# Row variance over 8192 columns: from chunk statistics on VectorE to a two-pass form, with the last two tiles' loads cut smaller

## Chip, cores, metric

One core of one Trainium2 chip. The metric is device time in microseconds of one execution, smaller is better. "Span" is the core's time in a profiled execution; in the runs here the measured time is 1.7 to 2.2 us above it. Runs of one call (one build, one chip, one sitting) agree within about 0.15%.

## The reference

```python
def setup_inputs():
    return {"x": np.random.randn(8192, 8192).astype(np.float32)}

def reference(x):
    return np.var(x, axis=1)
```

268 MB have to be read once and 32 KB written.

## The kernel before

A tile is 128 partitions of 2 rows each, 8.39 MB. There are 32 tiles and three tile buffers. For each row VectorE takes statistics of twelve 512-column chunks, ScalarE sums the last 2048 columns and their squares around the first chunk's mean, GpSimd turns these into a thirteenth entry, and VectorE aggregates.

```python
    data = ctx.enter_context(tc.tile_pool(name="data", bufs=3))
    # ... J = 2, F = 512, C = 16, AC = 4, DC = 12, NA = 2048
    def row_stats(xt, j):
        # ...
        for c in range(DC):
            bn(st, c, xt[:, o + c * F : o + (c + 1) * F])
        k = st[:, 1:2]
        src = xt[:, o + DC * F : o + m]
        nc.scalar.activation(out=junk, in_=src, func=ACTF.Identity, bias=k, scale=-1.0,
                             accum_out=s12[:, 0:1])
        nc.scalar.activation(out=junk, in_=src, func=ACTF.Square, bias=k, scale=-1.0,
                             accum_out=s12[:, 1:2])
        # ... six small GpSimd operations, then bn_aggr on VectorE (finish)
    for t in range(NT - 1):
        xt = data.tile([P, J * m], FP32, name="xt")
        nc.sync.dma_start(out=xt, in_=x_t[t])              # one load a tile
        # ... row_stats for both rows, finish one row later
    # last tile: row 0 whole, row 1 in pieces
    nc.sync.dma_start(out=xt[:, 0:m], in_=x_t[t, :, 0:m])
    pieces = [4096, 2048, 1024, 512, 256, 256]
    # ... row 0 as above, row 1 in 17 chunks on VectorE alone
    with nc.allow_non_contiguous_dma(reason="two values per partition"):
        nc.sync.dma_start(out=out_last[t], in_=var_last)   # 128 writes of 8 bytes
```

## Time and profile before

| | before |
|---|---|
| time, median | 648.35 us (648.18 to 649.04, 4 runs) |
| span of the profiled run | 646.7 us |
| last piece of the input landed | 629.2 us |
| VectorE done | 642.5 us |

The prediction shows the profile's lines. The table's third line is not on the page: it is from the trace's record of the semaphores that loads raise, where each load shows sixteen steps, one for each of the 16 DMA engines by my reading (the trace does not name them). The sixteenth step is taken as the landing: the last load's first step is at 622.49, its sixteenth at 629.20. The view of stretches puts the end in two lines (columns: stretch in us and its length, then busy us and number of instructions of PE, PEld, DVE, ACT and POOL, TensorE's clock, DMA share, GB/s):

```profile
609.60:629.20 19.60, 0.42 (x1) 0.12 (x1) 19.54 (x34) 12.46 (x13) 2.15 (x13) 1.00 0.66 273
629.20:642.60 13.40, 0.42 (x1) 0.13 (x1) 13.27 (x25) 0.42 (x3) 0.56 (x3) 1.00 0.01 2
```

After 629.2 nothing comes in any more (2 GB/s), and VectorE is busy for 13.27 of 13.4 us. That is the part of a load-bound kernel that can be shortened.

### The profile page before, as it was taken

The numbers are of one execution on the slowest core, as the hardware profiler recorded it, in microseconds if no ns is written. First come the engines' busy times: TensorE is split into PE (matmuls) and PEld (weight loads), VectorE is DVE, ScalarE is ACT, GpSimd is POOL, SyncE is SP. The second block draws the span as 40 slices with busy tenths as digits, with TensorE's granted clock in tenths as the row PEclk, the third lists the DMA queues.
The fourth block names the chain that finished last, engine by engine and source line by source line (L and its number), as shares of the span: only waits on it lengthen the run. The fifth ranks groups of instructions, "written<-read, shape, count | busy, mean of one in ns | idle before, by whom it ended". The sixth has DMA issues, their size and how long they took to land.

```text
span 646.7 us, 1908 instructions
## 1 busy us (share of the span) xinstructions
PE 0.8 (0%) x2; PEld 0.3 (0%) x2; DVE 485.3 (75%) x838; ACT 265.5 (41%) x255; POOL 58.9 (9%) x384
## 2 busy tenths in 40 slices
PE   0000000000000000000000000000000000000000
PEld 0000000000000000000000000000000000000000
DVE  0576797776897776887767987677977677976797
ACT  0443455343454342454343554333553434552450
POOL 0010110010100010101010100101100101100110
DMA  9999999999999999999999999999999999999950
GB/s 389 454 417 426 454 426 417 454 439 405 450 446 401 450 450 398 450 450 409 438 446 422 430 442 439 409 450 454 397 450 446 401 450 446 398 447 454 395 209 3
DMA packets 5663, 268.59 MB, mean 415 GB/s; under 512 B 753, under 2 KB 1040, under 8 KB 1296
## 3 DMA queue, kind: packets, MB, share of 16 engines
q1 hardware_dynamic: 5648, 268.47, 96.2%
q14 instruction: 15, 0.12, 0.1%
HBM read 268.44 MB, written 0.03 MB: 415 GB/s over the span
## 4 chain that ended last, share of the span: by engine, by line
DMA 72%; DVE 26%; issue 1%; SPq 0%; DVEq 0%
DMA xt<-in_x_dram 72%; DVE st L50 25%; DVE stl L50 1%; DVE mv L127 0%; DVE mv L78 0%; DVE mv L124 0%; SPq L84 0%; DVEq L50 0%; DVE var_last L128 0%
## 5 line engine op out<-in xcount | busy, mean ns | idle before, releaser
L50 DVE BATCH_NORM_STATS2 st<-xt 128x6 f32<-128x512 f32 x756 | 451.6, 678 | 157.2 <-DMA xt<-in_x_dram 157.2
L63 ACT ACTIVATE junk<-xt,st 128x2048 f32<-128x2048 f32 x63 | 124.2, 1971 | 339.4 <-DVE st L50 339.4
L65 ACT ACTIVATE junk<-xt,st 128x2048 f32<-128x2048 f32 x63 | 124.2, 1971 | 2.0
L69 POOL TENSOR_SCALAR tmp<-s 128x1 f32<-128x1 f32 x63 | 12.0, 190 | 387.9 <-ACT junk L63 387.9
L78 DVE BATCH_NORM_AGGREGATE mv<-st 128x2 f32<-128x75 f32 x62 | 25.8, 457 | 0.0
L73 POOL TENSOR_TENSOR st<-s,tmp 128x1 f32<-128x1 f32 x63 | 11.9, 189 | 100.6 <-ACT junk L65 100.6
L79 POOL COPY var_all<-mv 128x1 f32<-128x1 f32 x62 | 11.4, 183 | 79.0 <-DVE mv L78 79.0
L71 POOL TENSOR_TENSOR st<-st,tmp 128x1 f32<-128x1 f32 x63 | 11.9, 189 | 5.2
L72 POOL TENSOR_TENSOR tmp<-s,tmp 128x1 f32<-128x1 f32 x63 | 11.9, 189 | 0.0
L63 ACT ACTIVATION_READ_ACCUMULATOR junk<-xt,st 128x1 f32 x63 | 11.7, 186 | 0.0
L65 ACT ACTIVATION_READ_ACCUMULATOR junk<-xt,st 128x1 f32 x63 | 11.7, 186 | 0.0
L63 ACT ACT_TABLE_LOAD x1 | 1.3, 1283 | 22.7 <-DMA xt<-in_x_dram 22.7
L50 DVE BATCH_NORM_STATS2 stl<-xt 128x6 f32<-128x512 f32 (+1 forms) x17 | 9.6, 645 | 0.0
L68 POOL MEMSET st<- 128x1 f32 x63 | 6.2, 98 | 0.3 <-POOLq L145 0.3
L110 ACT COPY vs<-vp 31x128 f32<-31x128 f32 x2 | 0.5, 254 | 3.3 <-PE vp L109 3.3
L109 PE MATMUL vp<-ident,var_all 128*31 128x128 f32 x2 | 0.8, 420 | 631.7 <-POOL var_all L79 631.7
L127 DVE BATCH_NORM_AGGREGATE mv<-stl 128x2 f32<-128x102 f32 x1 | 0.6, 616 | 0.0
L109 PEld LDWEIGHTS vp<-ident,var_all 128*31 128x31 f32 x2 | 0.3, 126 | 632.0 <-POOL var_all L79 632.0
L124 DVE BATCH_NORM_AGGREGATE mv<-st 128x2 f32<-128x75 f32 x1 | 0.5, 481 | 0.0
L125 POOL COPY var_last<-mv 128x1 f32<-128x1 f32 x1 | 0.2, 183 | 1.3 <-DVE mv L124 1.3
masks.py:199 POOL TENSOR_SCALAR_AFFINE_SELECT ident<-ident 128x128 f32<-128x128 f32 x1 | 0.3, 292 | 0.1
masks.py:197 POOL MEMSET ident<- 128x128 f32 x1 | 0.2, 204 | 0.0
(5 smaller groups left out, 0.6 us busy)
## 6 DMA issues: line engine op xcount, KB each, us to landing
xt<-in_x_dram SPq DMA_DIRECT2D x1, 4096.0 KB, 34.9
xt<-in_x_dram SPq DMA_DIRECT2D x1, 2048.0 KB, 39.5
xt<-in_x_dram SPq DMA_DIRECT2D x1, 1024.0 KB, 41.4
xt<-in_x_dram SPq DMA_DIRECT2D x1, 512.0 KB, 42.2
xt<-in_x_dram SPq DMA_DIRECT2D x31, 44.5
xt<-in_x_dram SPq DMA_DIRECT2D x1, 256.0 KB, 42.4
xt<-in_x_dram SPq DMA_DIRECT2D x2, 128.0 KB, 40.6
out_dram<-vs SPq DMA_DIRECT2D x1, 31.0 KB
```

Of the source, the lines that this page charges most:

```text
L50: nc.vector.bn_stats(out=st[:, at * 6 : at * 6 + 6], in_=src)
L63: nc.scalar.activation(out=junk, in_=src, func=ACTF.Identity, bias=k, scale=-1.0, accum_out=s12[:, 0:1])
L65: nc.scalar.activation(out=junk, in_=src, func=ACTF.Square, bias=k, scale=-1.0, accum_out=s12[:, 1:2])
L68: nc.gpsimd.memset(st[:, b : b + 1], float(NA))
L69: nc.gpsimd.tensor_scalar(out=tmp[:, 0:1], in0=s12[:, 0:1], scalar1=1.0 / NA, scalar2=0.0, op0=ALU.mult, op1=ALU.add)
L71: nc.gpsimd.tensor_tensor(out=st[:, b + 1 : b + 2], in0=k, in1=tmp[:, 0:1], op=ALU.subtract)
L72: nc.gpsimd.tensor_tensor(out=tmp[:, 1:2], in0=s12[:, 0:1], in1=tmp[:, 0:1], op=ALU.mult)
L73: nc.gpsimd.tensor_tensor(out=st[:, b + 2 : b + 3], in0=s12[:, 1:2], in1=tmp[:, 1:2], op=ALU.subtract)
L78: nc.vector.bn_aggr(out=mv, in_=st)
L79: nc.gpsimd.tensor_copy(out=var_all[:, j, t : t + 1], in_=mv[:, 1:2])
L109: nc.tensor.transpose(vp, var_all[:, j, 0 : NT - 1], ident)
L127: nc.vector.bn_aggr(out=mv, in_=stl[:, 0 : i * 6])
```

## The change

The intent: one VectorE instruction sums a row by adding its halves as 4096 pairs, ScalarE divides by the row's length and then sums the squared differences in place. VectorE's work for a tile falls (from 14.34 us for 24 statistics to two sums), so that it is ready when the last pieces come. The last two tiles' loads are cut smaller; the last tile keeps chunk statistics, with 2048 columns of its last row on ScalarE.

```diff
+    def row_sum(s, i, src, w):
+        nc.vector.scalar_tensor_tensor(
+            out=pair[:, 0 : w // 2], in0=src[:, 0 : w // 2], scalar=1.0, in1=src[:, w // 2 : w],
+            op0=ALU.mult, op1=ALU.add, accum_out=s[:, i : i + 1])
+    def row_sq(s, k, src, t, j):
+        # (k == 1)
+        nc.scalar.activation(out=mean, in_=s[:, 0:1], func=ACTF.Identity, scale=1.0 / m)
+        nc.scalar.activation(out=src, in_=src, func=ACTF.Square, bias=mean, scale=-1.0,
+                             accum_out=ssq[:, j, t : t + 1])
     for t in range(NT - 1):
         xt = data.tile([P, J * m], FP32, name="xt")
-        nc.sync.dma_start(out=xt, in_=x_t[t])
+        if last:                                   # tile 30
+            for lo, hi in ((0, m), (m, m + H), (m + H, 2 * m)):
+                nc.sync.dma_start(out=xt[:, lo:hi], in_=x_t[t, :, lo:hi])
+        else:
+            nc.sync.dma_start(out=xt, in_=x_t[t])
         # ... row_sum, row_sq for both rows (the last row of tile 30 in two sums)
-    nc.sync.dma_start(out=xt[:, 0:m], in_=x_t[t, :, 0:m])
-    pieces = [4096, 2048, 1024, 512, 256, 256]
+    for w in [2048] * 6 + [1024, 1024, 512, 512, 512, 256, 256]:
         nc.sync.dma_start(out=xt[:, lo : lo + w], in_=x_t[t, :, lo : lo + w])
         # ... tile 31: row 0 in 16 chunks, row 1 in 13 chunks on VectorE, 2048 columns on ScalarE
```

More of the change, by code (lines that the diff above doesn't have):

```diff
@@ L27 @@
     NT = n // (P * J)
-    C = m // F
-    AC = 4
-    DC = C - AC
-    NA = AC * F
-    T3 = 3
+    H = m // 2
     x_t = x.rearrange("(t p j) f -> t p (j f)", p=P, j=J)
@@ L39 @@
     data = ctx.enter_context(tc.tile_pool(name="data", bufs=3))
-    stats = ctx.enter_context(tc.tile_pool(name="stats", bufs=6))
-    small = ctx.enter_context(tc.tile_pool(name="small", bufs=6))
+    stats = ctx.enter_context(tc.tile_pool(name="stats", bufs=1))
+    small = ctx.enter_context(tc.tile_pool(name="small", bufs=4))
     singles = ctx.enter_context(tc.tile_pool(name="singles", bufs=1))
     psum = ctx.enter_context(tc.tile_pool(name="psum", bufs=1, space=bass.MemoryType.PSUM))
-    var_all = singles.tile([P, J, NT], FP32)
+    ssq = singles.tile([P, J, NT], FP32)
@@ L46 @@
     var_last = singles.tile([P, J], FP32)
-    junk = psum.tile([P, NA], FP32)
-    def bn(st, at, src):
-        nc.vector.bn_stats(out=st[:, at * 6 : at * 6 + 6], in_=src)
-    def row_stats(xt, j):
-        st = stats.tile([P, DC * 6 + T3], FP32)
-        s12 = small.tile([P, 2], FP32)
-        tmp = small.tile([P, 2], FP32)
-        o = j * m
-        for c in range(DC):
-            bn(st, c, xt[:, o + c * F : o + (c + 1) * F])
-        k = st[:, 1:2]
-        src = xt[:, o + DC * F : o + m]
-        nc.scalar.activation(out=junk, in_=src, func=ACTF.Identity, bias=k, scale=-1.0,
-                             accum_out=s12[:, 0:1])
-        nc.scalar.activation(out=junk, in_=src, func=ACTF.Square, bias=k, scale=-1.0,
-                             accum_out=s12[:, 1:2])
-        b = DC * 6
-        nc.gpsimd.memset(st[:, b : b + 1], float(NA))
-        nc.gpsimd.tensor_scalar(out=tmp[:, 0:1], in0=s12[:, 0:1], scalar1=1.0 / NA, scalar2=0.0,
-                                op0=ALU.mult, op1=ALU.add)
-        nc.gpsimd.tensor_tensor(out=st[:, b + 1 : b + 2], in0=k, in1=tmp[:, 0:1], op=ALU.subtract)
-        nc.gpsimd.tensor_tensor(out=tmp[:, 1:2], in0=s12[:, 0:1], in1=tmp[:, 0:1], op=ALU.mult)
-        nc.gpsimd.tensor_tensor(out=st[:, b + 2 : b + 3], in0=s12[:, 1:2], in1=tmp[:, 1:2], op=ALU.subtract)
-        return st
@@ L76, in finish @@
-    def finish(st, t, j):
-        mv = small.tile([P, 2], FP32)
-        nc.vector.bn_aggr(out=mv, in_=st)
-        nc.gpsimd.tensor_copy(out=var_all[:, j, t : t + 1], in_=mv[:, 1:2])
-    pending = []
+    pair = psum.tile([P, H], FP32)
+    ident = singles.tile([P, P], FP32)
+    make_identity(nc, ident)
+    def row_sum(s, i, src, w):
+        nc.vector.scalar_tensor_tensor(
+            out=pair[:, 0 : w // 2], in0=src[:, 0 : w // 2], scalar=1.0, in1=src[:, w // 2 : w],
+            op0=ALU.mult, op1=ALU.add, accum_out=s[:, i : i + 1])
@@ new lines, in row_sq @@
+    def row_sq(s, k, src, t, j):
+        mean = small.tile([P, 1], FP32, name="mean")
+        if k == 1:
+            nc.scalar.activation(out=mean, in_=s[:, 0:1], func=ACTF.Identity, scale=1.0 / m)
+        else:
+            parts = small.tile([P, 4], FP32, name="parts")
+            nc.scalar.activation(out=parts[:, 0:k], in_=s[:, 0:k], func=ACTF.Identity, scale=1.0 / m,
+                                 accum_out=mean)
+        nc.scalar.activation(out=src, in_=src, func=ACTF.Square, bias=mean, scale=-1.0,
+                             accum_out=ssq[:, j, t : t + 1])
@@ L82 @@
     for t in range(NT - 1):
         xt = data.tile([P, J * m], FP32, name="xt")
-        nc.sync.dma_start(out=xt, in_=x_t[t])
-        for j in range(J):
-            st = row_stats(xt, j)
-            pending.append((st, t, j))
-            if len(pending) > 1:
-                finish(*pending.pop(0))
+        rows = [xt[:, j * m : (j + 1) * m] for j in range(J)]
+        last = t == NT - 2
+        if last:
+            for lo, hi in ((0, m), (m, m + H), (m + H, 2 * m)):
+                nc.sync.dma_start(out=xt[:, lo:hi], in_=x_t[t, :, lo:hi])
+        else:
+            nc.sync.dma_start(out=xt, in_=x_t[t])
@@ L92 @@
+        for j in range(J):
+            s = small.tile([P, 2], FP32, name="s")
+            if last and j == J - 1:
+                row_sum(s, 0, rows[j][:, 0:H], H)
+                row_sum(s, 1, rows[j][:, H:m], H)
+                row_sq(s, 2, rows[j], t, j)
+            else:
+                row_sum(s, 0, rows[j], m)
+                row_sq(s, 1, rows[j], t, j)
     t = NT - 1
     xt = data.tile([P, J * m], FP32, name="xt")
-    nc.sync.dma_start(out=xt[:, 0:m], in_=x_t[t, :, 0:m])
-    pieces = [4096, 2048, 1024, 512, 256, 256]
@@ L96 @@
-    lo = m
-    for w in pieces:
+    lo = 0
+    for w in [2048] * 6 + [1024, 1024, 512, 512, 512, 256, 256]:
         nc.sync.dma_start(out=xt[:, lo : lo + w], in_=x_t[t, :, lo : lo + w])
         lo += w
-    st = row_stats(xt, 0)
-    finish(*pending.pop(0))
-    ident = singles.tile([P, P], FP32)
-    make_identity(nc, ident)
     vs = singles.tile([NT - 1, P, J], FP32)
     for j in range(J):
-        vp = psum.tile([NT - 1, P], FP32, name="vp")
-        nc.tensor.transpose(vp, var_all[:, j, 0 : NT - 1], ident)
-        nc.scalar.copy(vs[:, :, j], vp)
+        vp = pair[0 : NT - 1, j * F : j * F + P]
+        nc.tensor.transpose(vp, ssq[:, j, 0 : NT - 1], ident)
+        nc.scalar.mul(vs[:, :, j], vp, 1.0 / m)
@@ L111 @@
     nc.sync.dma_start(out=out_tj[0 : NT - 1], in_=vs)
-    stl = stats.tile([P, (C + 1) * 6], FP32, name="stl")
-    lo, i = m, 0
-    while lo < 2 * m:
-        w = F
-        if 2 * m - lo <= 512:
-            w = 256
-        bn(stl, i, xt[:, lo : lo + w])
-        lo += w
-        i += 1
-        if i == 2:
-            mv = small.tile([P, 2], FP32)
-            nc.vector.bn_aggr(out=mv, in_=st)
-            nc.gpsimd.tensor_copy(out=var_last[:, 0:1], in_=mv[:, 1:2])
-    mv = small.tile([P, 2], FP32)
@@ L127, with bn @@
-    nc.vector.bn_aggr(out=mv, in_=stl[:, 0 : i * 6])
-    nc.vector.tensor_copy(out=var_last[:, 1:2], in_=mv[:, 1:2])
+    def bn(st, i, lo, w):
+        nc.vector.bn_stats(out=st[:, i * 6 : i * 6 + 6], in_=xt[:, lo : lo + w])
+    st0 = stats.tile([P, m // F * 6], FP32, name="st0")
+    for c in range(m // F):
+        bn(st0, c, c * F, F)
+    mv0 = small.tile([P, 2], FP32, name="mv0")
+    NA = 2048
+    st1 = stats.tile([P, 13 * 6 + 3], FP32, name="st1")
+    b = 13 * 6
+    s12 = small.tile([P, 2], FP32, name="s12")
@@ new lines @@
+    tmp = small.tile([P, 2], FP32, name="tmp")
+    nc.gpsimd.memset(st1[:, b : b + 1], float(NA))
+    bn(st1, 0, m, F)
+    k = st1[:, 1:2]
+    src = xt[:, m + NA : m + 2 * NA]
+    junk = pair[:, NA : 2 * NA]
+    nc.scalar.activation(out=junk, in_=src, func=ACTF.Identity, bias=k, scale=-1.0, accum_out=s12[:, 0:1])
+    nc.scalar.activation(out=junk, in_=src, func=ACTF.Square, bias=k, scale=-1.0, accum_out=s12[:, 1:2])
+    nc.gpsimd.tensor_scalar(out=tmp[:, 0:1], in0=s12[:, 0:1], scalar1=1.0 / NA, scalar2=0.0,
+                            op0=ALU.mult, op1=ALU.add)
@@ new lines @@
+    nc.gpsimd.tensor_tensor(out=st1[:, b + 1 : b + 2], in0=k, in1=tmp[:, 0:1], op=ALU.subtract)
+    nc.gpsimd.tensor_tensor(out=tmp[:, 1:2], in0=s12[:, 0:1], in1=tmp[:, 0:1], op=ALU.mult)
+    nc.gpsimd.tensor_tensor(out=st1[:, b + 2 : b + 3], in0=s12[:, 1:2], in1=tmp[:, 1:2], op=ALU.subtract)
+    for i in range(1, 4):
+        bn(st1, i, m + i * F, F)
+    nc.vector.bn_aggr(out=mv0, in_=st0)
+    nc.gpsimd.tensor_copy(out=var_last[:, 0:1], in_=mv0[:, 1:2])
+    lo = m + 2 * NA
+    for i, w in enumerate([512] * 7 + [256, 256]):
+        bn(st1, 4 + i, lo, w)
+        lo += w
@@ L129 @@
+    mv1 = small.tile([P, 2], FP32, name="mv1")
+    nc.vector.bn_aggr(out=mv1, in_=st1)
+    nc.vector.tensor_copy(out=var_last[:, 1:2], in_=mv1[:, 1:2])
     with nc.allow_non_contiguous_dma(reason="two values per partition"):
```

## The prediction

> **What bounds the kernel now.** I read the busy shares first, then the slices, the DMA queues, the chain that ended last, and last the timeline of the end.
>
> ```profile
> PE 0.8 (0%) x2; PEld 0.3 (0%) x2; DVE 485.3 (75%) x838; ACT 265.5 (41%) x255; POOL 58.9 (9%) x384
> ...
> DMA  9999999999999999999999999999999999999950
> ...
> q1 hardware_dynamic: 5648, 268.47, 96.2%
> q14 instruction: 15, 0.12, 0.1%
> ...
> DMA 72%; DVE 26%; issue 1%; SPq 0%; DVEq 0%
> ...
> L50 DVE BATCH_NORM_STATS2 st<-xt 128x6 f32<-128x512 f32 x756 | 451.6, 678 | 157.2 <-DMA xt<-in_x_dram 157.2
> L63 ACT ACTIVATE junk<-xt,st 128x2048 f32<-128x2048 f32 x63 | 124.2, 1971 | 339.4 <-DVE st L50 339.4
> ```
>
> No engine is the bound over the run: VectorE is busy 75%, and waits 157.2 us for loads. The DMA slices stand at 9 until the last two. 268.4 MB of input have to come in, and the queue is full for 96.2% of the span. The 26% that the chain gives VectorE are mostly not worth removing: the chain alternates between a load that waited for a buffer and the VectorE work that freed that buffer, but loads are queued two deep, so that work lies beside transfers. Only the two ends of the span are exposed: the first tile's load (22.7 us until VectorE starts) and whatever follows the last landing.
>
> ```profile
> 565.02 44.55 DMA xt<-in_x_dram
> ...
> 609.66 7.29 DVE st L50 x13
> ...
> 633.39 8.33 DVE stl L50 x15
> 641.72 0.02 issue
> 641.74 0.62 DVE mv L127
> 642.36 0.03 issue
> 642.39 0.15 DVE var_last L128
> ```
>
> From 609.66, when tile 30 (the last but one) is complete, VectorE works without a pause until 642.54. It has 24 chunks of tile 30, 12 of tile 31's row 0 and 17 of row 1 to do, and while VectorE needs 14.34 us for a whole tile plus 0.83 for its aggregates, the arrival of the tile 31 pieces doesn't hold it back at all. The trace's record of the loads' semaphores, which one step per DMA engine raises, says when data was there: the fifteenth engine delivers its last piece of tile 31 at 625.1, the sixteenth and last at 629.2. So 13.3 us of VectorE work stand behind the last landing, and then 4.2 us of output (642.54 to 646.7).
>
> **A second loss, in the same record.** The first engine delivers a tile every 19.35 us. The last engine trails it by 0.55 us at tile 0 and by 6.9 at tile 29, and this grows in seven jumps, the first of 0.6 and the others of about 0.95 us. The packets of the instruction queue (8 KB each, about 0.31 us) fall at such jumps (60.6, 143.7, 241.4, 319.8, 398.2, 495.9, 574.2 us). VectorE has 838 instructions, one jump for each 120. My reading is that VectorE's instruction fetches go through one DMA engine that also carries data, and every tile waits for that engine. This is an inference, not shown.
>
> [...] This trace has no two-input VectorE operation[...]; its 512-column statistic, one input, starts every 14.34/24 = 0.598 us[...].
>
> **The change, main loop.** Removed for tiles 0 to 30: 12 chunk statistics and an aggregate a row on VectorE, two 2048-column activations on ScalarE and six small operations on GpSimd. Added per row: one VectorE sum of 4096 pairs with an accumulator read [...], one tiny ScalarE activation for the mean [...], and one Square over 8192 in place [...]. [...] None of this moves the stream: the main loop gains nothing directly.
>
> **The change, stream.** VectorE drops to 63 sums, 63 accumulator reads, 29 statistics and 3 others, 158 instructions: one fetch after the start instead of seven. ScalarE has about 200. I expect a lag of 1.5 to 2.5 us of the last engine in place of 6.7. Against that stand more pieces: in the trace each load costs the first engine some 0.07 us over its bytes (2048 columns come every 2.49 us, where bytes alone make 2.42), and there are 16 loads for tiles 30 and 31 where there were 8, so +0.6. The first engine ends at 622.5 now, then at 623.1, and the last landing falls at 623.1 + 2 = about 625.0 (now 629.2).
>
> **The change, end.** Tile 29 lands at about 584.8, tile 30 at 604.8.
> - ScalarE: [...] The transposes' copies (each 0.25, and one wait for TensorE) bring 621.3. Then the two 2048 activations for the share of the last row that it took, 2 x 2.15: 625.6. GpSimd's last step 0.5: 626.1.
> - VectorE: [...] Tile 31's row 0 comes in four pieces, 2.49 us apart, with 4 x 0.598 = 2.39 of work each: it keeps pace. In row 1 the second piece is ScalarE's, which gives it about 2.4 us of slack, and the later pieces shrink from 1024 to 256 columns. After the last landing one 256 statistic is left (the 256 form shows 0.416): 625.4.
> - So the last aggregate starts at the later of 625.4 and 626.1, say 626.3. Aggregate 0.62, copy 0.18: 627.1. The output's 4.2: span 631.3, against 646.7. The measured time was 1.8 above the span (648.52 against 646.7): 633.1. Gain 15.2 us: 4.2 from the earlier last landing, 11 from the shorter work behind it.
>
> I predict **633.2 us**, 2.3% below 648.34. The threshold of 2% lies near 635.6.
>
> **Rivals.**
> - [...]
> - **ScalarE becomes the bound of the end.** Its chain from tile 29 is only 0.7 us longer than the loads' in my sum; each 0.3 us more a row makes 1.2 us. [...]
> - **The fetches do not shrink, or the lag has another cause.** Then the last landing is 629.8; VectorE has little behind it: 630.2 + 0.8 + 4.2 + 1.8 = 637.0, 1.7% faster.
> - **The stream gets thin,** since buffers come free later and the piecewise loads wait for earlier semaphores (in the new order the loads after the eighth of tile 31 wait for pieces of that tile itself). Each is still issued over 5 us before its turn, so I expect nothing; if it bites, 1 to 3 us.
>
> **Range and chances.** [...] Together: faster by over 2% 0.68, within 2% 0.30, slower 0.02. The range that should hold eight of ten is 630.5 to 638.
>
> **What would show it.** [...] In the waits, VectorE and ScalarE both wait for loads or for each other in every tile, and the load queue waits for ScalarE with DMA slices still at 9. In the semaphore record, the last engine less than 3 us behind the first. In the timeline, the last Square of tile 30 ending near 620, the ScalarE share near 625.6, and VectorE idle just before its last pieces or its last aggregate. A DMA slice under 9 before the end, or VectorE busy without a pause from tile 30 on, would make the prediction wrong.

The sum came to 633.1 us, written as 633.2. Terms of it: what VectorE takes for the sum of a row, and what ScalarE takes for a row. They led from tile 29's landing (584.8) to the 621.3 of ScalarE's line. The time to spare in the main loop rested on them too, and so did a rival with a slower sum, given 18%, and the split of the chances by it. The trace of the changed kernel shows these terms: 4433 ns for the sum and 141 for its accumulator read, 195 for the mean, 7123 for the Square; from tile 29's first sum to the end of the fourth row it took 34.1 us (585.47 to 619.57).

## The result, and the profile after

634.38 us median (634.12 to 634.73, 4 runs) against 648.35. The ratio is 0.9783 (95% interval 0.9766 to 0.98): faster by 2.2%. Ratios here are the mean time of one kernel's fast runs over the mean of the other's of the same rounds, so not quite the ratio of the medians quoted. A second call with the unaltered changed kernel gave 633.49 us and 0.9765.

The page of the changed kernel: busy shares, slices, queues, chain and the two main groups (their lines end in busy us, mean ns of one, and the engine's idle time before them with what ended it).

```profile
PE 0.8 (0%) x2; PEld 0.3 (0%) x2; DVE 297.2 (47%) x158; ACT 462.4 (73%) x194; POOL 1.6 (0%) x12
...
DMA  9999999999999999999999999999999999999994
...
q1 hardware_dynamic: 6800, 268.47, 98.5%
q14 instruction: 5, 0.04, 0.0%
...
ACT 42%; DMA 40%; DVE 15%; another core or an unknown queue 2%; issue 0%; SPq 0%; DVEq 0%
...
L62 ACT ACTIVATE xt<-xt,mean 128x8192 f32<-128x8192 f32 x62 | 441.6, 7123 | 2.0
L49 DVE SCALAR_TENSOR_TENSOR pair<-xt 128x4096 f32<-128x4096 f32 (+1 forms) x63 | 275.0, 4366 | 328.6 <-ACT xt L62 236.3
```

The last group mixes two widths. The view of the tile `pair` shows its durations apart (ns, shortest/median/longest):

```profile
L49 DVE SCALAR_TENSOR_TENSOR pair<-xt x63: 2299/4433/4434, 22.6 to 605.0; 128x4096 f32<-128x4096 f32 x61, 128x2048 f32<-128x2048 f32 x2
```

The work moved from VectorE (75% to 47%) to ScalarE (41% to 73%), and neither bounds the run: the DMA slices now stand at 9 to the last but one. The chain gives ScalarE 42%, which must not be read as cost. The chain walks from a load to the Square that freed its buffer, and that Square ran beside other loads. In the queue's own waits this shows as a long list of waits for ScalarE with the DMA engines busy throughout (columns: us in total, times, longest us):

```profile
SPq L73 <- ACT xt L62: 275.3, 27, 10.3
```

The end, from the timeline of the changed kernel (columns: start, us, engine, line, operation, output<-input, count, idle time before and what ended it):

```profile
612.35 7.12 ACT L62 ACTIVATE xt<-xt,mean 128x8192 f32<-128x8192 f32 x1
...
621.79 5.01 DVE L101 BATCH_NORM_STATS2 st<-xt 128x6 f32<-128x512 f32 x9 [0.84 <-DMA xt<-in_x_dram]
...
624.61 0.19 ACT L120 ACTIVATION_READ_ACCUMULATOR pair<-xt,st 128x1 f32 x1
624.93 0.19 POOL L125 TENSOR_TENSOR st<-s,tmp 128x1 f32<-128x1 f32 x1 [1.57 <-ACT pair L120]
626.90 0.52 DVE L135 BATCH_NORM_AGGREGATE mv<-st 128x2 f32<-128x81 f32 x1
627.46 0.15 DVE L136 COPY var_last<-mv 128x1 f32<-128x1 f32 x1
```

VectorE now waits for pieces (0.84 us before its last nine statistics). The chain's end splits these nine where the second 1024-column piece lands, at 623.05 (start, us, what):

```profile
623.08 3.73 DVE st L101 x7
```

The last piece landed at 625.67, VectorE was done at 627.61. So 1.94 us stand behind the last landing where there were 13.34.

Where 13.8 us of span came from: the last landing came 3.5 us earlier (629.20 to 625.67), the work behind it is 11.4 us shorter, and the output after it is 1.1 us longer (4.19 to 5.34 us from VectorE's end to the span's end).

### The profile page after: what moved, and what is told of

Its sections match the earlier page's. It is cut to its first block, busy times and chain, and to the rows that moved or that the text cites. A ratio compares the mean times of both kernels' runs of the same rounds, so it can differ in the third digit from the quotient of the medians.

```text
span 632.9 us, 589 instructions
## 1 busy us (share of the span) xinstructions
PE 0.8 (0%) x2; PEld 0.3 (0%) x2; DVE 297.2 (47%) x158; ACT 462.4 (73%) x194; POOL 1.6 (0%) x12
## 4 chain that ended last, share of the span: by engine, by line
ACT 42%; DMA 40%; DVE 15%; another core or an unknown queue 2%; issue 0%; SPq 0%; DVEq 0%
ACT xt L62 41%; DMA xt<-in_x_dram 40%; DVE pair L49 14%; ACT mean L57 1%; DVE st L101 1%; DVE mv L135 0%; SPq L73 0%; SPq L71 0%; DVEq L49 0%; DVE var_last L136 0%; DVEq L135 0%
## 5 line engine op out<-in xcount | busy, mean ns | idle before, releaser
L62 ACT ACTIVATE xt<-xt,mean 128x8192 f32<-128x8192 f32 x62 | 441.6, 7123 | 2.0
L49 DVE SCALAR_TENSOR_TENSOR pair<-xt 128x4096 f32<-128x4096 f32 (+1 forms) x63 | 275.0, 4366 | 328.6 <-ACT xt L62 236.3
L57 ACT ACTIVATE mean<-s 128x1 f32<-128x1 f32 x61 | 11.9, 195 | 159.0 <-DVE pair L49 159.0
L101 DVE BATCH_NORM_STATS2 st<-xt 128x6 f32<-128x512 f32 (+1 forms) x29 | 17.3, 660 | 1.6 <-DMA xt<-in_x_dram 1.6
L62 ACT ACTIVATION_READ_ACCUMULATOR xt<-xt,mean 128x1 f32 x62 | 11.6, 187 | 0.0
L49 DVE DVE_READ_ACCUMULATOR pair<-xt 128x1 f32 x63 | 8.9, 141 | 0.0
L121 POOL TENSOR_SCALAR tmp<-s 128x1 f32<-128x1 f32 x1 | 0.2, 193 | 3.9 <-ACT pair L119 3.9
L125 POOL TENSOR_TENSOR st<-s,tmp 128x1 f32<-128x1 f32 x1 | 0.2, 191 | 1.6 <-ACT pair L120 1.6
L123 POOL TENSOR_TENSOR st<-st,tmp 128x1 f32<-128x1 f32 x1 | 0.2, 192 | 0.1
L124 POOL TENSOR_TENSOR tmp<-s,tmp 128x1 f32<-128x1 f32 x1 | 0.2, 192 | 0.0
## 6 DMA issues: line engine op xcount, KB each, us to landing
xt<-in_x_dram SPq DMA_DIRECT2D x3, 256.0 KB, 13.8
```

Of the source, the lines that this page charges most:

```text
L49: nc.vector.scalar_tensor_tensor(out=pair[:, 0 : w // 2], in0=src[:, 0 : w // 2], scalar=1.0, in1=src[:, w // 2 : w], op0=ALU.mult, op1=AL ...
L57: nc.scalar.activation(out=mean, in_=s[:, 0:1], func=ACTF.Identity, scale=1.0 / m)
L62: nc.scalar.activation(out=src, in_=src, func=ACTF.Square, bias=mean, scale=-1.0, accum_out=ssq[:, j, t : t + 1])
L101: nc.vector.bn_stats(out=st[:, i * 6 : i * 6 + 6], in_=xt[:, lo : lo + w])
L121: nc.gpsimd.tensor_scalar(out=tmp[:, 0:1], in0=s12[:, 0:1], scalar1=1.0 / NA, scalar2=0.0, op0=ALU.mult, op1=ALU.add)
L123: nc.gpsimd.tensor_tensor(out=st1[:, b + 1 : b + 2], in0=k, in1=tmp[:, 0:1], op=ALU.subtract)
```

## The experiments

Ten kernels ran. All gave correct results. They ask three things. Is it the arithmetic or the cutting of loads that takes work from behind the last landing? Is the last DMA engine late because of instruction fetches? What is left at the end?

### 1 and 2. The loads alone, and the arithmetic alone

The kernel before, with the changed kernel's loads:

```diff
-        nc.sync.dma_start(out=xt, in_=x_t[t])
+        cuts = ((0, m), (m, m + m // 2), (m + m // 2, 2 * m)) if t == NT - 2 else ((0, 2 * m),)
+        for lo, hi in cuts:
+            nc.sync.dma_start(out=xt[:, lo:hi], in_=x_t[t, :, lo:hi])
-    pieces = [4096, 2048, 1024, 512, 256, 256]      # and row 0 whole
+    pieces = [2048] * 6 + [1024, 1024, 512, 512, 512, 256, 256]
```

> The kernel before, with only the changed kernel's loads for the last two tiles (3 for tile 30, 13 for tile 31); all arithmetic as before. Theory (most of the gain is that VectorE no longer stands behind the last landing, and the load cutting is what does it; the two-pass arithmetic adds only the shorter lag of one DMA engine): last landing 629.2 + 0.6 = 630, VectorE done some 2 us later, 637 of span, 638.5 us, ratio to before 0.985. Rival (the last tiles need the emptier VectorE of the two-pass scheme): VectorE still 5 us or more behind the last landing, 642 us or more, ratio 0.99 or above.

The changed kernel, with the loads of before:

```diff
-        last = t == NT - 2
+        last = False
-    for w in [2048] * 6 + [1024, 1024, 512, 512, 512, 256, 256]:
+    for w in [8192, 4096, 2048, 1024, 512, 256, 256]:
```

> The changed kernel with the loads of before (tile 30 whole, tile 31 as row 0 and then 4096, 2048, 1024, 512, 256, 256). Theory (cutting the loads is what takes work from behind the last landing): VectorE is at row 0 of tile 31 only from about 614.5, does 29 statistics from there, ends near 633, span 638.5, 640 us, ratio to before 0.987. Rival (the two-pass arithmetic alone makes the end short): 635 us or less, ratio 0.979.

Measured in one call, beside a kernel before of 648.71 us; the lower right cell is from the two other calls:

| | loads of before | loads of the change |
|---|---|---|
| chunk statistics | 648.71 | 644.39 (ratio 0.9932) |
| two passes | 638.81 (ratio 0.9845) | 634.38 and 633.49 (0.9783 and 0.9765) |

Each half gains about the same whether the other is there or not: the loads 4.3 to 5.3 us, the arithmetic 9.9 to 10.9. For the arithmetic alone the theory held: VectorE reached row 0 of tile 31 at 614.46 (614.5 expected), ended at 632.48 (near 633), and the time was 638.81 (640). For the loads alone my theory fell (638.5 expected). The stretches after the last landing, with the columns as above, first for the loads alone (landing at 629.65), then for the arithmetic alone (624.34):

```profile
629.70:638.10 8.40, 0.00 (x0) 0.00 (x0) 8.29 (x16) 0.00 (x0) 0.00 (x0) 1.00 0.00 0
```
```profile
624.30:632.50 8.20, 0.00 (x0) 0.00 (x0) 8.04 (x16) 4.42 (x5) 0.86 (x5) 1.00 0.01 4
```

Sixteen VectorE instructions are still to be done then, in either kernel: each half alone leaves 8.1 to 8.4 us behind the last landing, and only both together leave 1.94. So some 5 of the 10 us that the arithmetic gains alone are work behind the landing (13.34 to 8.14), and the rest is the earlier landing. In the timeline of the loads alone VectorE starts on tile 29 at 590.25, when that whole tile has landed, and from there works without a gap through tiles 29, 30 and 31. It is a tile late before the small pieces come, and at 15 us a tile against 19.35 it catches up by only about 4 us a tile. That is a reason to cut earlier, not yet one for other arithmetic.

### 3. Chunk statistics, with loads cut earlier

The arithmetic of before, tiles 27 to 29 by rows, tile 30 in four, tile 31 as in the change, and ScalarE taking 2048 columns of the last row as in the change (that code is the changed kernel's, shown shortened):

```diff
-        nc.sync.dma_start(out=xt, in_=x_t[t])
+        cuts = 1 if t < NT - 5 else 2 if t < NT - 2 else 4
+        for lo in range(0, 2 * m, 2 * m // cuts):
+            hi = lo + 2 * m // cuts
+            nc.sync.dma_start(out=xt[:, lo:hi], in_=x_t[t, :, lo:hi])
+    # tile 31, row 1: 13 chunks on VectorE, columns 2048 to 4095 on ScalarE
```

> The arithmetic of before (bn_stats with ScalarE's quarter) in all tiles, but with loads cut earlier: tiles 27 to 29 by rows, tile 30 in four, tile 31 in the changed kernel's 13 pieces, and ScalarE takes 2048 columns of the last row too. The first trial, with only tiles 30 and 31 cut, showed VectorE still a tile behind because tile 29 came whole. Theory (VectorE at 15.2 us a tile keeps pace with loads of 19.35 once it sees them in small pieces; the two-pass arithmetic then gains only the shorter lag of the last DMA engine): last landing 630, VectorE done 2 us later, span 637, 638.5 us, ratio to before 0.984. Rival (one-pass arithmetic can't be made to end with the loads): 642 us or more.

Measured: 638.02 us, ratio 0.9835 (0.9821 to 0.9848). The last landing is at 630.01, and VectorE is done 1.94 us later, the same distance as in the changed kernel:

```profile
610.00:630.00 20.00, 0.42 (x1) 0.12 (x1) 16.92 (x30) 12.83 (x13) 2.50 (x14) 1.00 0.70 281
630.00:632.00 2.00, 0.00 (x0) 0.00 (x0) 1.81 (x5) 0.00 (x0) 0.00 (x0) 1.00 0.00 0
```

So the 11 us behind the last landing don't need the two passes. Chunk statistics keep pace with the loads once VectorE sees them in time and ScalarE takes its share of the last row; how much each of these two edits gave was not taken apart. What two passes have over this kernel is the rest, 3.6 to 4.5 us, and their last landing is 4.3 to 4.8 us earlier (625.67 and 625.18 against 630.01).

### 4 to 6. Why the last landing is earlier: instruction fetches

In the changed kernel VectorE has 158 instructions in place of 838, and the instruction queue has 5 packets in place of 15. To test the link, instructions without use were added to the changed kernel where their engine waits anyway; nothing else changed.

```diff
                 row_sum(s, 0, rows[j], m)
+                if j == J - 1:
+                    for _ in range(20):             # third kernel: 10 on vector and 10 on gpsimd
+                        nc.vector.tensor_copy(out=pad_vector, in_=s[:, 0:1])   # second kernel: nc.gpsimd
```

> The changed kernel with 20 one-column copies on VectorE a tile (600 in all) after each tile's second sum, where VectorE waits over 10 us anyway. Theory (instructions of VectorE are fetched through one DMA engine that also carries data, each 120 or so costing that engine 0.95 us): five more jumps, the last engine trails by some 6.5 us at the end in place of 2, the last landing at 630, 639 us, ratio to before 0.985. Rival (the lag came from VectorE's own traffic or from the loads, not from the number of instructions): lag still 2 us, 634.4 us, ratio 0.978.

> The same 20 one-column copies a tile, on GpSimd, which has nothing else to do there. Theory (fetching counts, whichever engine the instructions are for): again about five more jumps of the last DMA engine, 639 us, ratio to before 0.985. Rival (only VectorE's instructions or its memory accesses do it): lag 2 us and 634.4 us.

> The changed kernel with 10 one-column copies a tile on VectorE and 10 on GpSimd, in place of 20 on one of them. Theory (each engine's instructions are fetched over a DMA engine of its own, and the loads wait for the one that trails most, so the maximum counts and not the sum): two or three jumps of 0.97 for VectorE, two or three of 0.65 for GpSimd on another DMA engine; lag of the last engine 3 us, last landing 626, 635 us, ratio 0.979. Rival (both go over the same DMA engine, so they add up): lag 4.5 us, 636.5 us.

The lines of the instruction queue on the pages of the first, second and third of these kernels, in this order (packets, MB, share):

```profile
q14 instruction: 9, 0.07, 0.0%
```
```profile
q14 instruction: 10, 0.08, 0.0%
```
```profile
q14 instruction: 10, 0.08, 0.0%
```

What they do to the loads, by how far the last DMA engine trails the first in the semaphore record (us):

| kernel | tile 0 | tile 12 | tile 20 | tile 29 | last landing | time, us (ratio) |
|---|---|---|---|---|---|---|
| before | 0.55 | 3.0 | 5.0 | 6.9 | 629.2 | 648.35 |
| change | 0.6 | 1.1 | 1.1 | 1.3 | 625.67 | 634.38 (0.9783), 633.49 (0.9765) |
| change + 20 on VectorE | 0.65 | 1.7 | 3.7 | 5.7 | 628.75 | 637.67 (0.983) |
| change + 20 on GpSimd | 0.7 | 1.5 | 2.1 | 3.4 | 626.21 | 634.71 (0.9784) |
| change + 10 on each | 0.6 | 1.1 | 2.1 | 4.1 | 626.87 | 635.38 (0.9794) |

A packet of the instruction queue does not name the engine that it is for; below that is read from the times. Six hundred VectorE instructions, put where VectorE waits, bring the lag back, and 3.3 to 4.2 us of time with it (some 0.35 us of this lies outside the span: this kernel's time is 2.1 us above its span, the changed kernel's 1.8). The trace dates it: with 20 on VectorE, 8 KB packets of the instruction queue start at 70.2, 167.8, 265.5, 363.3 and 461.0, 97.7 us or five tiles apart, and at 553.9, and the lag steps up by 0.94 to 1.0 us at each but the first, which gave 0.2 (presumably its DMA engine was not the last until then; the trace does not name the engines). GpSimd shows that it doesn't take VectorE's memory traffic: its copies do it too (3.4 us of lag at tile 29 against 1.3), but its steps are 0.65 us and not the 0.97 that I had taken from VectorE, and the time was 634.71 where I expected 639. With GpSimd's copies only the lag is shown, not a cost in time: at the last piece the lag is 3.3 us against 1.8 without them, the landing 0.5 to 1.0 us later, and the time 0.3 to 1.2 us longer, in other calls.

With 10 on each, VectorE fetched four times (104.2, 259.8, 415.6 and 571.4 us) and GpSimd three times (114.0, 349.2, 582.1). If both went over one DMA engine, 0.6 + 3.5 + 3 x 0.65 = 6.0 us of lag would be due; VectorE's own four steps, of 0.5, 1.0, 1.0 and 1.0, give 4.1, and 4.1 is measured. That speaks for two different DMA engines, with the sixteenth step set by the one that trails most; it is inferred from these sums. The kernel before agrees without added instructions: there the fifteenth landing of a tile trails the first by 0.80, 1.46, 2.08 and 2.74 us from tiles 4, 12, 20 and 28 on, each after one of GpSimd's four packets (91.9, 247.4, 402.9 and 560.7 us), while VectorE's seven steps alone make up the 6.9 us of the sixteenth. (Both figures that I wrote beforehand counted too few fetches.) In VectorE's own work no stall shows: the 24 statistics of a tile took 14.33 to 14.34 us in each of the 31 tiles of the kernel before. Not settled: why the lag steps up by 0.97 us at a packet of 0.31 to 0.35 us for VectorE, and by 0.65 for GpSimd.

### 7 and 8. What is left at the end

The changed kernel with the last 256 values as one row:

```diff
-    nc.vector.tensor_copy(out=var_last[:, 1:2], in_=mv1[:, 1:2])
-    with nc.allow_non_contiguous_dma(reason="two values per partition"):
-        nc.sync.dma_start(out=out_last[t], in_=var_last)
+    row = singles.tile([1, P, J], FP32)
+    for j, mv in ((0, mv0), (1, mv1)):
+        rp = pair[0:1, (2 + j) * F : (2 + j) * F + P]
+        nc.tensor.transpose(rp, mv[:, 1:2], ident)
+        nc.vector.tensor_copy(out=row[:, :, j], in_=rp)
+    nc.sync.dma_start(out=out_tj[t : t + 1], in_=row)
```

> The changed kernel with its last 256 values turned by TensorE into one row and written as one kilobyte from one partition, in place of 128 writes of 8 bytes. Theory (the output's 4.4 us from issue to landing are the many small writes): TensorE and the copy cost 0.9 us, [...]633.5 us, ratio to the changed kernel 0.998. Rival (the landing time is fixed, whatever is written): 635.3 us.

Measured: 631.32 us (631.18 to 631.52), ratio to before 0.9731. The queue's wait for the output, in the changed kernel and in this one:

```profile
SPq L164 <- DMA out_dram<-var_last: 3.8, 1, 3.8
```
```profile
SPq L166 <- DMA out_dram<-row: 0.6, 1, 0.6
```

The columns are those of the queue's waits above. The turning took 0.7 us (the last transpose starts at 627.08 and the copy ends at 627.77; 0.9 was expected), and the time fell by more than expected (631.32 for 633.5). From VectorE's end to the span's end it is 1.97 us in place of 5.34. In the record the row landed within 1.1 us of its issue, the 128 small writes in 4.4. Whether their size or their number is the reason is not shown.

The changed kernel with the last two 1024-column loads as four of 512:

```diff
-    for w in [2048] * 6 + [1024, 1024, 512, 512, 512, 256, 256]:
+    for w in [2048] * 6 + [512] * 7 + [256, 256]:
```

> The changed kernel with the last row's two loads of 1024 columns cut into four of 512. Theory (VectorE reads a column about as fast as it comes, so at the end it stands behind by one piece: the 1024 piece): last landing 0.1 later, VectorE behind it by 1.4 instead of 1.9 us, 633.9 us. Rival (ScalarE's share or the output sets the end): 634.4 us.

Measured: 632.88 us, ratio 0.9757. VectorE ends 1.53 us behind the last landing in place of 1.94, as the theory has it. The gain in time isn't shown: the unaltered changed kernel came to 633.49, and 0.6 us is less than two calls of one kernel differ by.

### 9 and 10. Both together, and the change once more

The ninth kernel has both edits, the tenth none.

> The two last trials together: the last values written as one row, and the last row's 1024-column loads cut into 512. Both gains are behind the last landing and follow one another on the same path (VectorE's backlog, then the output), so they add: 634.4 - 3.1 - 1.5 = 629.8, ratio to before 0.971. If the output of the row overlaps with nothing and the finer cut only moved a wait, 631.3.

> The changed kernel unaltered, beside the other on the same chip. Its first profile shows all DMA engines losing 0.7 us between 119 and 178 us, which none of the variants' profiles shows so far. If that belongs to the run and not to the kernel, the first engine ends near 623.1 here and the loads come each 19.35 us throughout; time 634.4 us.

Measured: 631.30 us (ratio 0.9733) and 633.49 us (0.9765). The sum of the two gains did not come: both edits together are no faster than the row alone (631.32). In its profile VectorE's aggregate starts at 626.05 against 626.51 with the row alone, but this stays below what the times resolve. The 0.7 us that all DMA engines lost between 119 and 178 us in the first profile are not there in the second profile, where tiles reach the first DMA engine each 19.35 us save two, at 19.47 and 19.44. They belong to that run. The row alone is the version to keep: 2.7% below before.

## Why the prediction was right

633.2 us was predicted, 634.38 measured; the range held. Step by step:

- **The time of the sum**, the fork that the chances hung on: 4433 ns for 4096 pairs (the groups' mean of 4366 mixes in two of 2048), 141 for the accumulator read. With 2299 ns for 2048 pairs that is 1.04 ns a pair and 0.17 us fixed. The rival with a slower sum is out.
- **ScalarE's row**: 7123 ns for the Square, and 7.34 us from one Square to the next (570.89 to 578.23); the term in the sum was somewhat larger. ScalarE's tail was 0.8 us early (624.80 for 625.6). ScalarE never became the bound, and that rival is out.
- **The stream**: tile 29 landed at 585.35 (584.8 predicted), tile 30 at 604.86 (604.8), the last piece at 625.67 (625.0). The lag was 1.8 us for 2, although VectorE fetched twice after its start (225.7 and 608.8 us) and not once. The cause behind it, marked as inferred, is now supported by the added instructions (5.7 us of lag at tile 29 with 600 more on VectorE, 1.3 without).
- **Mis-sized term 1, VectorE's backlog**: "After the last landing one 256 statistic is left", ready at 625.4. The last statistic ended at 626.80. VectorE reads columns in about the time that they take to arrive (2.39 us for 2048 against 2.49), so it hardly catches up with what it has not read when a large piece lands: the second 1024 piece landed at 623.05, 2.6 us before the end, with 3.7 us of work in it and behind it. So VectorE set the end, and not ScalarE as my sum had it. That the sum's 626.3 for the last aggregate came so near to the 626.90 measured is partly luck: the 626.1 for ScalarE's path (its last step ended at 625.12) was about 1 us too late, and stood in for a VectorE that was 1.4 us too early.
- **Mis-sized term 2, the output**: 4.2 us were carried over from before, 5.34 measured (4.76 in the second call). Its 128 small writes took 4.4 and 3.8 us to land, and 2.8 before. I didn't see that this term could vary, nor that it was the largest one left. Why it is longer here is open: it was 2.7 to 2.9 in three kernels (before, two passes with the loads of before, chunk statistics cut earlier) and 3.5 to 4.4 in those with the change's loads, and no run took this apart.
- **What I read into the gain**: 4.2 us from the landing and 11 behind it were predicted, 3.5 and 11.4 measured, less 1.1 of output. The prediction did not say that the 11 could be had with the old arithmetic and earlier cuts. The third experiment shows it.
- **Two slips of the text**: its sum ends at 633.1 and not 633.2, and 2% below 648.34 is 635.4 and not 635.6.

## What to carry to other kernels

In a kernel bound by loads, look first at what is still to do when the last byte has landed, and cut loads early enough that the engine behind them isn't a whole tile late when the small pieces come; with chunk statistics the last two tiles were too late here (8.4 us behind the last landing, against 1.94 with tiles 27 to 30 cut as well and ScalarE taking part of the last row). Instruction fetches weighed on the loads here: 600 added VectorE instructions made the last landing 3.1 to 3.6 us later (628.75 against 625.67 and 625.18), and of two ways with the same 1.94 us behind the last landing, the one with 158 VectorE instructions in place of 834 let the input land 4.3 to 4.8 us earlier. And write the last result as one contiguous row if a transpose is at hand (2.2 to 3.1 us here).
